# Attention on one core: where the fold of a head's halves stands in the ScalarE and VectorE queues

## The chip, the cores and the metric

The kernel runs on one core of one Trainium2 chip, as a single launch. The metric is the device time of that launch in microseconds (us). One core has five engines with an instruction queue each: TensorE (PE in the profile, with its weight loads as PEld), VectorE (DVE), ScalarE (ACT), GpSimd (POOL) and SyncE (SP), which here only issues DMAs.

## The reference, cut to what matters

Two layers of a transformer trunk over 1024 tokens of 1024 features, in float32. Each layer has an attention stage and a dense SwiGLU stage. The first layer (called A here) has windowed attention with 12 query heads, the second (B) a two-dimensional neighbourhood attention with 12; both have 4 more heads over 256 memory tokens.

```python
def reference(x, mem, ...):
    for i in range(DEPTH):                       # 2 layers
        h = rmsnorm(x, norm_mix[i])
        y_tok = windowed_gqa(...) if i % 2 == 0 else neighbourhood_attn(...)   # 12 heads of 64
        y_mem = memory_attn(qm, mk, mv)                                        # 4 heads of 64
        x = x + jnp.concatenate([y_tok, y_mem], axis=-1) @ w_out[i]
        h = rmsnorm(x, norm_ffn[i])
        gu = h @ w_gate_up[i]
        x = x + (jax.nn.silu(gu[..., :D_FF]) * gu[..., D_FF:]) @ w_down[i]
    return rmsnorm(x, norm_final)
...
    p = jax.nn.softmax(s)                        # in each head
    o = jnp.einsum('bkgniu,bnukd->bnikgd', p, vband)
```

## The kernel before

Every float32 operand of a matmul is kept as a high part, rounded to the matmul's type by ACT (`hi`, L107), and a low part, the rest, which DVE makes (`lo`, L110). Products are sums of such parts. In attention, a value tile holds a head's values as 64 high and 64 low columns side by side, so the product of probabilities and values comes out on 128 partitions: the upper 64 rows belong to the low part. To finish a head they have to be added to the lower 64. This is the fold: ACT copies the upper rows to a temporary `yt` (L819) and DVE adds the lower rows and `yt` into the result tile `y` (L830).

The attention stage works on "halves": one head (16 of them) and one half of the tokens (512, in four blocks of 128), so 32 halves per layer and 64 in all. For each half there are three jobs:

- `scores` (L739): per block two matmuls into a PSUM bank `S` (there are two such banks), a DVE pass that adds the bias and takes the row minimum (L757; for memory heads a maximum, L752), an exponential on ACT (L761 or L753); then a reciprocal on DVE (L769, L771) and the scaling of the four blocks by POOL (L774).
- `turn` (L782): per block two or three transposes on PE into a PSUM bank `pT` (L789; three banks, tag `T`), then `ph` on ACT (L793) and `pl` on DVE (L794), which are `hi` and `lo` of the transposed block. The fourth block of a half needs the bank of the first one, so its transposes wait for the first `pl`.
- `mix` (L797): the matmuls of `ph` and `pl` with the values (L809) into the PSUM bank `O`, and at its end the fold. There is one `O` bank (`ps_o`, one buffer), so the first L809 matmul of a half waits for the fold of the half before. At the second half of an odd head the finished pair of heads, `y`, is stored to `y_d` by a DMA on SP's queue (L832), and read back later (`load_y`, L938).

The main loop (L963 to L1000) traces, for each i, the scores of half i+1, the mix of half i-1 with its fold, and the turn of half i. Between the steps of these jobs it pulls pieces of other work: the projections of later heads (`mm`, L141), and towards the end of the stage the first pieces of the output projection (`po`, L141; `out_units`, L945). The last heads have only `po` to be filled with; these halves are called the tail here.

The order of the trace isn't yet the order in the queues. The Tile framework's scheduler goes through the traced instructions with that order as priority, and puts those first whose inputs and buffers its own cost model holds to be ready. Then each engine runs its queue in order. Semaphores are set where an instruction depends on one of another engine.

Of the kernel before, what the change touches and what calls it, by code (L numbers as in the profile page):

```python
# [41 lines left out]
def trunk_kernel(ctx: ExitStack, tc: tile.TileContext, a: dict, out: bass.AP):  # L42
# [17 lines left out]
    nc = tc.nc  # L60
# [37 lines left out]
    def temp(name="t2k", n=HS):  # L98
        t = phase[0].tile([P, HS], F32, tag="t2k", name=name, bufs=phase[1])
        return t[:, :n] if n != HS else t  # L100
# [3 lines left out]
        return phase[0].tile([P, D], F32, tag="raw", name=name, bufs=phase[2])  # L104

    def hi(dst, src):
        nc.scalar.copy(dst, src)  # L107

    def lo(dst, src, h, eng=None):
        (eng or nc.vector).tensor_tensor(dst, src, h.bitcast(F32), op=ALU.subtract)  # L110

    def load_w(src, tag="whl", bufs=3, eng=None, name="w", pool=wp, parts=1, raw=None):
        if raw is None:
# [33 lines left out]
    def run(g):  # L147
        for _ in g:
            pass
# [392 lines left out]
    for layer in range(2):  # L542
        is_a = layer == 0
        with tc.tile_pool(name=f"ap{layer}", bufs=1, reuse_waits="tile") as ap:
# [163 lines left out]
                return lambda qb: t[:, 1 if qb in (0, 7) else 0]  # L708


            biases, ys = {}, {}

            class Half:
                def __init__(self, h, u):
# [67 lines left out]
                def turn(self):  # L782
                    self.ph = ap.tile([P, 12, P], F32R, tag="ph", bufs=2, name="ph")
                    self.pl = ap.tile([P, 12, P], F32R, tag="pl", bufs=2, name="pl")
                    step = 4 if self.mem else 2
                    for p, (qb, b0, b1, n) in zip(self.p, self.blocks):
                        tr = ps_t.tile([P, HS], F32, tag="T", name="pT")
                        for j in range(b1 - b0):
                            nc.tensor.transpose(tr[:, j * P : (j + 1) * P], p[:, j * P : (j + 1) * P], ident)  # L789
                        s0 = self.slot(b0, qb)  # L790
                        sl = slice(s0, s0 + step * (b1 - b0 - 1) + 1, step)
                        src = tr[:, :n].rearrange("p (j q) -> p j q", q=P)
                        hi(self.ph[:, sl], src)  # L793
                        lo(self.pl[:, sl], src, self.ph[:, sl])  # L794
                        yield

                def mix(self):  # L797
                    u = self.u
                    if u == 0 and not self.odd:
                        ys[self.pair] = ap.tile([P, S], F32, tag="y", bufs=2, name="y")  # L800
                    y = ys[self.pair]
                    o = ps_o.tile([P, HS], F32, tag="O", name="O")
                    js = sorted({j for _, b0, b1, _ in self.blocks for j in range(b0, b1)})
                    for j in js:
                        qbs = [qb for qb, b0, b1, _ in self.blocks if b0 <= j < b1]
                        s0, w = self.slot(j, qbs[0]), len(qbs)
                        c0 = (qbs[0] - 4 * u) * P
                        for t in (self.ph, self.pl):
                            nc.tensor.matmul(  # L809
                                o[:, c0 : c0 + w * P], self.value(j),  # L810
                                t[:, s0 : s0 + w].rearrange("p j q -> p (j q)"),
                                start=j == js[0] and t is self.ph, stop=j == js[-1] and t is self.pl,
                                skip_group_check=True,
                            )
                        yield

                    t = temp("yt")
                    rs = slice(HD, P) if self.odd else slice(0, HD)
                    nc.scalar.copy(t[:HD], o[HD:])  # L819
                    if self.mem:  # L820
                        d, o_, t_ = y[rs, u * HS : (u + 1) * HS], o[:HD], t[:HD]
                    elif is_a:
                        v = lambda z: z.rearrange("p (r f c) -> p f r c", f=2, c=32)
                        d = y[rs].rearrange("p (f r c) -> p f r c", f=2, c=32)[:, :, 8 * u : 8 * u + 8]
                        o_, t_ = v(o[:HD]), v(t[:HD])
                    else:
                        v = lambda z: z.rearrange("p (s r c) -> p r s c", s=4, c=SC)
                        d = y[rs, u * HS : (u + 1) * HS].rearrange("p (r s c) -> p r s c", s=4, c=SC)
                        o_, t_ = v(o[:HD]), v(t[:HD])
                    nc.vector.tensor_tensor(d, o_, t_, op=ALU.add)  # L830
                    if u == 1 and self.odd and self.pair != last_pair:
                        nc.sync.dma_start(y_d[layer][self.pair], y)  # L832


            heads = [("m", 0), ("m", 1), *range(6), ("m", 2), ("m", 3), *range(6, NH)]
# [85 lines left out]
            def pull():  # L921
                try:
                    next(work)
                    taken[0] += 1
                except StopIteration:
                    pass
# [9 lines left out]
                yT[f][k] = t  # L936

            def load_y(f, k):  # L938
                raw = temp("yr")
                nc.sync.dma_start(raw, y_d[layer][k][:, f * HS : (f + 1) * HS])  # L940
                split_y(f, k, raw)
# [21 lines left out]
            for i in range(len(halves)):  # L963

                rate = 0.0
                for n in range(n0, len(units)):
                    if done[0] > n:
                        continue
                    left = (n + 1 - n0) * 2 * NK - taken[0]
                    rate = max(rate, left / max(dues[n] - i - 0.5, 0.5))  # L970
                if tail is not None:
                    rate = PACE[layer][i - len(halves)]
                if i == 0:
                    for _ in range(8):
                        pull()
                if is_a and 4 <= i < 4 + ROWS // 2:
                    for r in (2 * i - 8, 2 * i - 7):
                        spread_bias(r)
                jobs = []
                if i + 1 < len(halves):  # L980
                    jobs.append(halves[i + 1].scores())
                ahead = halves[min(i + 3, len(halves) - 1)].h
                if not isinstance(ahead, tuple) and ahead not in biases:
                    biases[ahead] = make_bias(ahead)
                if i > 0:
                    jobs.append(halves[i - 1].mix())
                jobs.append(halves[i].turn())
                for job in jobs:
                    for _ in job:
                        credit += rate / groups  # L990
                        while credit >= 1.0:
                            credit -= 1.0
                            pull()

                for n in range(n0, len(units)):
                    while dues[n] <= i + 1 and done[0] <= n:
                        pull()
                at[0] = i + 1
                if done[0] == len(units) and tail is None:
                    tail = work = out_units()  # L1000
            for _ in halves[-1].mix():
                pull()
            run(tail)
            for f in range(2):
                split_y(f, last_pair, ys[last_pair][:, f * HS : (f + 1) * HS])
# [731 lines left out]
```

## Time and profile before

| what | value |
|---|---|
| time, median of 3 runs | 2117.06 us (2116.92 to 2117.7) |
| time of the profiled execution | 2115.94 us |
| span of the profiled execution | 2114.2 us |
| DVE busy | 1524.6 us (72%) |
| ACT busy | 1077.9 us (51%) |
| POOL busy | 583.6 us (28%) |
| DMA, mean over the span | 136 GB/s |

The span is the time from the first to the last instruction in the trace; the time of an execution has 1.7 us around it. "Busy" is the share of the span in which an engine had at least one instruction running. A PE instruction's end is modelled, and one matmul starts while the one before still counts as running; so PE can be called busy while it waits for a short time. Such waits show in the distance from one start to the next.

In time, attention of layer A lies at about 80 to 335 us of the span and that of layer B at about 1060 to 1392 us; the tails begin at about 282 and 1364 us. The rest is the dense stage.

### The profile page before, as it was taken

Reading aid. Unit: us, or ns where it says so; the run is one execution under the profiler, and the core shown is the slowest. Engines: PE = TensorE matmul, PEld = TensorE weight load, DVE = VectorE, ACT = ScalarE, POOL = GpSimd, SP = SyncE. Lnnn points to the kernel's source line nnn. Section 1 sums busy time; section 2 is a strip of 40 time slices with the busy share of each in tenths; the row PEclk is TensorE's granted clock in tenths of the full one; section 3 lists DMA queues with packets and bytes.
Section 4 is the critical chain, followed back from the end, with each engine's and each line's share of the span. In section 5 each row is a group of like instructions: output and inputs, shape, how many; then the busy total and the mean of one; then the engine's idle time right before and its main releaser. Section 6 shows DMA issues by size and latency. Waiting matters only on the chain.

```text
span 2114.2 us, 29053 instructions
## 1 busy us (share of the span) xinstructions
PE 2092.7 (99%) x10318; PEld 1750.1 (83%) x10318; DVE 1524.6 (72%) x2474; ACT 1077.9 (51%) x2037; POOL 583.6 (28%) x615
## 2 busy tenths in 40 slices
PE   9999999999999999999999999999999999999998
PEld 8788888888888888888888888888888888888887
DVE  7687886987666667776766666677986666677675
ACT  6687775544434335344466666664543434344443
POOL 0344330334444430000233223203243444400001
PEclk9999999999999999999999999999999999999999
DMA  6421128332333227866232222275232333267662
GB/s 232 146 82 51 36 83 288 99 115 100 110 108 111 91 105 254 313 216 207 78 110 68 69 72 78 64 266 157 75 110 105 110 115 104 91 254 256 205 221 95
DMA packets 121778, 288.08 MB, mean 136 GB/s; under 512 B 12705, under 2 KB 21153, under 8 KB 121633
## 3 DMA queue, kind: packets, MB, share of 16 engines
q1 hardware_dynamic: 113744, 272.42, 38.4%
q10 hardware_dynamic: 7888, 13.79, 1.7%
q8 instruction: 82, 1.34, 0.3%
q14 instruction: 64, 0.52, 0.1%
HBM read 211.19 MB, written 68.95 MB: 133 GB/s over the span
## 4 chain that ended last, share of the span: by engine, by line
PE 80%; issue 12%; DVE 3%; ACT 2%; POOL 2%; DMA 1%; POOLq 0%; ACTq 0%; SPq 0%; DVEq 0%
PE X L1101 16%; PE Y L1101 16%; PE mm L141 15%; PE po L141 8%; PE X L1532 5%; PE Y L1532 4%; PE O L809 3%; PE S L746 3%; PE pT L789 3%; PE X L1183 2%; PE Y L1183 2%; PE mm L448 1%; ACT p L761 1%; POOL wS L1058 1%; POOL wf L110 1%
## 5 line engine op out<-in xcount | busy, mean ns | idle before, releaser
L1101 PE MATMUL Y<-hB,wgu 128*128 128x512 f32 x1056 | 255.5, 391 | 0.8 <-ACT c L1121 0.8
L1101 PE MATMUL X<-hB,wgu 128*128 128x512 f32 x1056 | 254.8, 391 | 0.0
L1532 PE MATMUL X<-hB,wd 128*128 128x512 f32 (+1 forms) x1092 | 243.2, 383 | 0.9 <-DVE x L1496 0.9
L110 DVE TENSOR_TENSOR wgu<-wS,wgu 128x1024 fp32r<-128x1024 f32 (+1 forms) x124 | 155.4, 1253 | 120.9 <-ACT wgu L107 120.7
L1532 PEld LDWEIGHTS X<-hB,wd 128*128 128x128 f32 x1092 | 200.2, 188 | 41.4 <-issue 1.7
L1101 PEld LDWEIGHTS Y<-hB,wgu 128*128 128x128 f32 x1056 | 196.8, 188 | 43.4 <-ACT c L1121 1.6
L1101 PEld LDWEIGHTS X<-hB,wgu 128*128 128x128 f32 x1056 | 196.0, 188 | 39.8
L774 POOL TENSOR_SCALAR p<-p,stat 128x384 f32<-128x384 f32 (+1 forms) x256 | 143.1, 579 | 308.7 <-DVE stat L771 213.4
L141 PE MATMUL mm<-hT,wqk 128*128 128x512 f32 x672 | 199.3, 405 | 0.0
L107 ACT CAST wgu<-wS 128x1024 fp32r<-128x1024 f32 (+1 forms) x124 | 114.3, 923 | 142.0 <-POOL wS L1058 124.6
L141 PE MATMUL po<-yT,wo 128*128 128x512 f32 x768 | 184.2, 393 | 0.0
L1532 PE MATMUL Y<-hB,wd 128*128 128x512 f32 x792 | 180.4, 389 | 0.0
L1532 PEld LDWEIGHTS Y<-hB,wd 128*128 128x128 f32 x792 | 148.6, 188 | 31.2 <-DVE x L1496 0.4
L244 POOL TENSOR_TENSOR nr<-nv,neg_half 128x4 f32<-128x4 f32 (+1 forms) x12 | 13.3, 1105 | 582.9 <-DVE nv L243 573.7
L141 PEld LDWEIGHTS po<-yT,wo 128*128 128x128 f32 x768 | 142.7, 188 | 28.8 <-DVE yT L110 0.2
L1101 PE MATMUL X<-hT,wgu 128*128 128x512 f32 x624 | 150.2, 391 | 0.0
L107 ACT CAST hB<-b_raw 128x512 fp32r<-128x512 f32 x154 | 89.4, 618 | 115.5 <-DMA b_raw<-b_d 100.3
L1058 POOL TENSOR_TENSOR wS<-wgu_raw 128x512 f32<-128x512 f32 x44 | 61.2, 1391 | 292.1 <-DVE wgu L110 292.1
L1101 PEld LDWEIGHTS X<-hT,wgu 128*128 128x128 f32 x624 | 116.8, 188 | 26.3
L761 ACT ACTIVATE p<-p,stat 128x256 f32<-128x256 f32 (+1 forms) x192 | 112.4, 587 | 48.1 <-DVE stat L757 46.0
L110 DVE TENSOR_TENSOR pl<-pT,ph 128x384 fp32r<-128x384 f32 (+1 forms) x256 | 119.0, 493 | 19.1 <-ACT ph L107 15.9
L110 DVE TENSOR_TENSOR hB<-b_raw,hB 128x512 fp32r<-128x512 f32 x154 | 99.9, 687 | 42.2 <-ACT hB L107 42.1
(201 smaller groups left out, 4248.1 us busy)
## 6 DMA issues: line engine op xcount, KB each, us to landing
wgu_raw<-in_w_gu SPq DMA_DIRECT2D x92, 512.0 KB, 3.7
wd_raw<-in_w_dn SPq DMA_DIRECT2D x70, 512.0 KB, 4.4
b_raw<-b_d SPq DMA_DIRECT2D x70, 512.0 KB, 5.4
b_d<-c SPq DMA_DIRECT2D x88, 256.0 KB, 2.1
b_d<-t SPq DMA_DIRECT2D x66, 256.0 KB, 2.2
wo_raw<-in_w_out SPq DMA_DIRECT2D x32, 512.0 KB, 3.5
xr_d<-x ACTq DMA_DIRECT2D x32, 256.0 KB, 2.5
xr<-xr_d SPq DMA_DIRECT2D x16, 512.0 KB, 6.1
```

Source lines behind the costliest of these rows:

```text
L107: nc.scalar.copy(dst, src)
L110: (eng or nc.vector).tensor_tensor(dst, src, h.bitcast(F32), op=ALU.subtract)
L141: nc.tensor.matmul(ps[:, :n], l, r, start=start and i == 0 and j == 0, stop=stop and i == len(order) - 1 and j == 2,)
L746: nc.tensor.matmul(s_[:, :n], Q[self.h][:, qb * P : (qb + 1) * P], k, start=j == 0, stop=j == 1)
L761: nc.scalar.activation(p[:, :n], p[:, :n], AF.Exp, bias=m1, scale=-1.0, accum_out=s1)
L774: nc.gpsimd.tensor_scalar(p[:, :n], p[:, :n], ri[:, i : i + 1], 1.0, op0=ALU.mult, op1=ALU.mult)
L789: nc.tensor.transpose(tr[:, j * P : (j + 1) * P], p[:, j * P : (j + 1) * P], ident)
L809: nc.tensor.matmul(o[:, c0 : c0 + w * P], self.value(j), t[:, s0 : s0 + w].rearrange("p j q -> p (j q)"), start=j == js[0] and t is self.p ...
L1058: sub = lambda o, p_, q_: nc.gpsimd.tensor_tensor(o, p_, q_, op=ALU.subtract)
L1101: nc.tensor.matmul(ps, l, r, start=n in (0, 1, 3, 6) and k == 0 and i == 0, stop=k == 3 and i == 2, skip_group_check=True,)
L1183: nc.tensor.matmul(bank[:, at : at + h2], l, r, start=start and k == 0 and i == 0, stop=stop and k == 1 and i == 2, skip_group_check=True,)
L1532: nc.tensor.matmul(bank[:, c], l, r, start=i in (0, 1, 3, 6) and p == 0 and n == 0, stop=p == HF - 1 and n == 2, skip_group_check=True,)
```

## The change

The fold is taken out of `mix` and becomes a method of its own, `fold`. The main loop calls it for half i-1 after the turn of half i, not before it. All that it traces is put into a context in which each traced instruction gets an order edge, without a semaphore, behind the last `ph` of the turn (if it runs on ACT) or the last `pl` (if on DVE). So the copy may not stand ahead of the four `ph` in ACT's queue, nor the add ahead of the four `pl` in DVE's. The store of `y` moves with it. The last half's fold has nothing to stand behind. An assertion makes sure that a pair is stored before it is read back.

```diff
@@ helpers
     def hi(dst, src):
-        nc.scalar.copy(dst, src)
+        return nc.scalar.copy(dst, src)
     def lo(dst, src, h, eng=None):
-        (eng or nc.vector).tensor_tensor(dst, src, h.bitcast(F32), op=ALU.subtract)
+        return (eng or nc.vector).tensor_tensor(dst, src, h.bitcast(F32), op=ALU.subtract)
@@ class Half, turn
-                        hi(self.ph[:, sl], src)
-                        lo(self.pl[:, sl], src, self.ph[:, sl])
+                        self.last = hi(self.ph[:, sl], src), lo(self.pl[:, sl], src, self.ph[:, sl])
                         yield
@@ class Half, end of mix
-
+                    self.o = o
+
+                def fold(self, behind=None):
+                    u, y, o = self.u, ys[self.pair], self.o
                     t = temp("yt")
                     rs = slice(HD, P) if self.odd else slice(0, HD)
+                    with ExitStack() as queued:
+                        for ins in behind.last if behind else ():
+                            queued.enter_context(tc.issue_after(ins.ins))
+                        self.add_halves(t, rs, u, y, o)
+                    if u == 1 and self.odd and self.pair != last_pair:
+                        nc.sync.dma_start(y_d[layer][self.pair], y)
+                        stored.add(self.pair)
+
+                def add_halves(self, t, rs, u, y, o):
                     nc.scalar.copy(t[:HD], o[HD:])
...
                     nc.vector.tensor_tensor(d, o_, t_, op=ALU.add)
-                    if u == 1 and self.odd and self.pair != last_pair:
-                        nc.sync.dma_start(y_d[layer][self.pair], y)
@@ load_y
+                assert k in stored
@@ main loop, after the jobs of half i
+                if i > 0:
+                    halves[i - 1].fold(halves[i])
...
             for _ in halves[-1].mix():
                 pull()
+            halves[-1].fold()
```

The queues outside the two attention stages stay as they were. Three places follow, first of before and then of the change. Tiles have a number behind their name here; the changed file's lines are shifted (L808 is L809 of before, L830 is L819, L841 is L830).

**Place 1, ACT, the steady part of layer A.** O_2076 belongs to the second half of head 3; the four `ph` behind it are those of the first half of head 4. Before:

```order
L767 ACTIVATE stat_2038<-stat_2038,sink_108 128x4
L107 CAST QS_1961<-scaled_2090 64x16x32
L107 CAST KH_1962<-scaled_2090 64x16x32
L819 COPY yt_2108<-O_2076 64x512
L107 CAST ph_2112<-pT_2114 128x2x128
L107 CAST ph_2112<-pT_2119 128x3x128
L107 CAST ph_2112<-pT_2128 128x3x128
L107 CAST ph_2112<-pT_2134 128x3x128
L761 ACTIVATE p_2144,stat_2140<-p_2144,stat_2140 128x256
```

The same place with the change:

```order
L767 ACTIVATE stat_2038<-stat_2038,sink_108 128x4
L107 CAST QS_1961<-scaled_2090 64x16x32
L107 CAST KH_1962<-scaled_2090 64x16x32
L107 CAST ph_2108<-pT_2110 128x2x128
L107 CAST ph_2108<-pT_2115 128x3x128
L107 CAST ph_2108<-pT_2124 128x3x128
L107 CAST ph_2108<-pT_2130 128x3x128
L830 COPY yt_2136<-O_2076 64x512
L761 ACTIVATE p_2144,stat_2140<-p_2144,stat_2140 128x256
```

The copy moved from ahead of the four `ph` to behind them; the casts of a projection (QS, KH) still stand ahead, and the next exponentials stand behind in both.

DVE at this place, before:

```order
L110 TENSOR_TENSOR KL_1963<-scaled_2090,KH_1962 64x16x32
L830 TENSOR_TENSOR y_1785<-O_2076,yt_2108 64x2x256
L110 TENSOR_TENSOR pl_2113<-pT_2114,ph_2112 128x2x128
L110 TENSOR_TENSOR pl_2113<-pT_2119,ph_2112 128x3x128
L110 TENSOR_TENSOR pl_2113<-pT_2128,ph_2112 128x3x128
L757 ISA p_2144,stat_2140<-S_2141,bias_1942,nsink_109 128x256
L757 ISA stat_2140 128x1
L110 TENSOR_TENSOR pl_2113<-pT_2134,ph_2112 128x3x128
```

With the change:

```order
L110 TENSOR_TENSOR KL_1963<-scaled_2090,KH_1962 64x16x32
L110 TENSOR_TENSOR pl_2109<-pT_2110,ph_2108 128x2x128
L110 TENSOR_TENSOR pl_2109<-pT_2115,ph_2108 128x3x128
L110 TENSOR_TENSOR pl_2109<-pT_2124,ph_2108 128x3x128
L110 TENSOR_TENSOR pl_2109<-pT_2130,ph_2108 128x3x128
L841 TENSOR_TENSOR y_1785<-O_2076,yt_2136 64x2x256
L757 ISA p_2144,stat_2140<-S_2141,bias_1942,nsink_109 128x256
```

The add moved behind the four `pl`, and now stands ahead of all L757 passes of the next scores; before, one of them came ahead of the last `pl`.

**Place 2, PE at the same place**, from the transposes of the first half of head 4 to the first matmul of its O. Before:

```order
L789 MATMUL pT_2128<-ident_106,p_1971 128x128 x3
L746 MATMUL S_2141<-KH_1012,QS_1344 128x256
L746 MATMUL S_2141<-KL_1013,QS_1344 128x256
L141 MATMUL mm_2104<-hT_586,wqk_1499 128x512 x2
L789 MATMUL pT_2134<-ident_106,p_1977 128x128 x3
L141 MATMUL mm_2104<-hT_586,wqk_1499 128x512
L746 MATMUL S_2150<-KH_1012,QS_1344 128x384
L746 MATMUL S_2150<-KL_1013,QS_1344 128x384
L141 MATMUL mm_2104<-hT_624,wqk_1499 128x512 x3
L746 MATMUL S_2156<-KH_1012,QS_1344 128x384
L746 MATMUL S_2156<-KL_1013,QS_1344 128x384
L809 MATMUL O_2179<-ph_2112,V_833 128x256
```

With the change:

```order
L789 MATMUL pT_2124<-ident_106,p_1971 128x128 x3
L789 MATMUL pT_2130<-ident_106,p_1977 128x128 x3
L746 MATMUL S_2141<-KH_1012,QS_1340 128x256
L746 MATMUL S_2141<-KL_1013,QS_1340 128x256
L141 MATMUL mm_2104<-hT_586,wqk_1499 128x512 x3
L746 MATMUL S_2150<-KH_1012,QS_1340 128x384
L746 MATMUL S_2150<-KL_1013,QS_1340 128x384
L141 MATMUL mm_2104<-hT_624,wqk_1499 128x512 x3
L141 MATMUL mm_2104<-hT_629,wqk_1499 128x512
L808 MATMUL O_2179<-ph_2108,V_833 128x256
```

The transposes of the fourth block moved up to those of the third, and more other matmuls stand between the last transpose and the first matmul of the next O.

**Place 3, ACT in the tail of layer A.** O_3485 is that of the first half of head 9, and the four `ph` are those of its second half. Before:

```order
L107 CAST ph_3499<-pT_3501 128x3x128
L107 CAST ph_3499<-pT_3507 128x3x128
L761 ACTIVATE p_3457,stat_3453<-p_3457,stat_3453 128x256
L761 ACTIVATE p_3463,stat_3453<-p_3463,stat_3453 128x384
L819 COPY yt_3496<-O_3485 64x512
L761 ACTIVATE p_3469,stat_3453<-p_3469,stat_3453 128x384
L761 ACTIVATE p_3475,stat_3453<-p_3475,stat_3453 128x384
L767 ACTIVATE stat_3453<-stat_3453,sink_108 128x4
L107 CAST ph_3499<-pT_3513 128x3x128
L107 CAST ph_3499<-pT_3519 128x2x128
```

With the change:

```order
L107 CAST ph_3496<-pT_3498 128x3x128
L761 ACTIVATE p_3457,stat_3453<-p_3457,stat_3453 128x256
L107 CAST ph_3496<-pT_3504 128x3x128
L107 CAST ph_3496<-pT_3510 128x3x128
L761 ACTIVATE p_3463,stat_3453<-p_3463,stat_3453 128x384
L761 ACTIVATE p_3469,stat_3453<-p_3469,stat_3453 128x384
L761 ACTIVATE p_3475,stat_3453<-p_3475,stat_3453 128x384
L767 ACTIVATE stat_3453<-stat_3453,sink_108 128x4
L107 CAST ph_3496<-pT_3516 128x2x128
L830 COPY yt_3521<-O_3485 64x512
```

Here the copy stood between two exponentials; now it stands behind all of them and behind the last `ph`.

More of the change, by code (lines that the diff above doesn't have):

```diff
@@ L708, in make_bias @@
                 return lambda qb: t[:, 1 if qb in (0, 7) else 0]
-            biases, ys = {}, {}
+            biases, ys, stored = {}, {}, set()
             class Half:
```

## The prediction

> **What bounds the kernel now.** I read the page first (busy shares, slices, granted clock), then busy time in four stretches, then who waits for whom, then the timeline around single folds. The page first:
>
> ```profile
> span 2114.2 us, 29053 instructions
> ...
> PE 2092.7 (99%) x10318; PEld 1750.1 (83%) x10318; DVE 1524.6 (72%) x2474; ACT 1077.9 (51%) x2037; POOL 583.6 (28%) x615
> ...
> PEclk9999999999999999999999999999999999999999
> ```
>
> PE is busy for all but 21.5 us of the span, with its full clock in every slice. An engine that is busy for 72% or 51% costs nothing by itself; the change can only win what PE loses to waits in the two attention stages. These are the steady part and the tail of layer A, then of layer B (columns: stretch and length, then busy us of PE, PEld, DVE, ACT, POOL):
>
> ```profile
> 80.00:262.00 182.00, 179.06 (x1009) 150.48 (x1007) 141.65 (x370) 137.72 (x374) 76.82 (x133) 1.00 0.19 60
> 262.00:335.00 73.00, 71.83 (x392) 59.31 (x391) 60.14 (x142) 56.54 (x132) 18.14 (x30) 1.00 0.40 140
> 1060.00:1364.00 304.00, 303.60 (x1639) 256.11 (x1637) 197.11 (x471) 194.42 (x486) 96.36 (x154) 1.00 0.25 73
> 1364.00:1392.00 28.00, 27.51 (x157) 23.12 (x156) 21.24 (x49) 20.07 (x46) 6.03 (x11) 1.00 0.58 190
> ```
>
> PE is idle for 2.9 + 1.2 + 0.4 + 0.5 = 5.0 us of these 587. What for, by the waits of PE's matmuls in 80 to 335 us, and by those of the whole span for the two instructions of the fold (total, times, longest):
>
> ```profile
> PE pT L789 <- DVE pl L110: 2.7, 7, 0.8
> ...
> DVE y L830 <- ACT yt L819: 37.4, 38, 3.2
> ACT yt L819 <- PE O L809: 35.0, 30, 2.8
> ```
>
> The two big numbers, 37.4 and 35.0 us, are idle time of ACT and DVE at the head of their queues, and not the gain: neither engine is the bound. They count only where what stands behind them makes PE late, and that is the 2.7 us: transposes that wait for a `pl` to free one of the three pT banks. This is how it comes about, at place 1:
>
> ```profile
> 172.90 0.86 PE L141 MATMUL mm<-hT,wqk 128*128 128x512 f32 x3
> 173.60 0.71 PE L789 MATMUL pT<-ident,p 128*128 128x128 f32 x5
> 174.06 0.94 PE L141 MATMUL mm<-hT,wqk 128*128 128x512 f32 x3
> 174.18 0.59 ACT L819 COPY yt<-O 64x512 f32<-64x512 f32 x1
> 174.49 0.96 DVE L110 TENSOR_TENSOR KL<-scaled,KH 64x512 fp32r<-64x512 f32 x1
> 174.79 1.14 ACT L107 CAST ph<-pT 128x256 fp32r<-128x256 f32 x3
> 175.41 0.62 PE L141 MATMUL mm<-hT,wqk 128*128 128x512 f32 x2
> 175.49 0.68 DVE L830 TENSOR_TENSOR y<-O,yt 64x512 f32<-64x512 f32 x1
> 176.20 1.35 DVE L110 TENSOR_TENSOR pl<-pT,ph 128x256 fp32r<-128x256 f32 x3
> 176.77 0.52 PE L789 MATMUL pT<-ident,p 128*128 128x128 f32 x3 [0.74 <-DVE pl L110]
> ```
>
> The first transposes are done at about 174, but ACT makes yt first, then DVE makes y, and only then the first `pl`; the fourth block's transposes start at 176.77. Two more things are in these rows. Three matmuls of 512 columns take 0.86 us together and one alone 0.39, so they start every 0.23 us: of each wait behind one, 0.16 us doesn't show as idle. And five transposes take 0.71, one 0.27: they start every 0.11 us, but a matmul follows the last of them after 0.03.
>
> **What goes: the waits for a pT bank.** I went through the start times of PE's matmuls and took each transpose that starts over 0.12 us later than its usual distance, 0.15 us behind the end of a `pl` that a fold had delayed. There are 10 in layer A (4.7 us) and 3 in B (0.8 us). The first and the last, each with the matmuls ahead:
>
> ```profile
> 135.98 0.48 PE L141 MATMUL mm<-hT,wqm 128*128 128x512 f32 x1
> 136.65 0.41 PE L789 MATMUL pT<-ident,p 128*128 128x128 f32 x2 [0.19 <-DVE pl L110]
> ...
> 1331.00 0.86 PE L141 MATMUL mm<-hT,wv 128*128 128x512 f32 x3
> 1332.04 0.41 PE L789 MATMUL pT<-ident,p 128*128 128x128 f32 x2 [0.18 <-DVE pl L110]
> ```
>
> The first: 136.65 - 135.98 - 0.23 = 0.44 us. The last: the third matmul starts at 1331.47, so 0.34. Together 5.5 us, the upper bound; the lower is the idle that the view itself shows, 2.7.
>
> With the change, yt (0.58) and y (0.68) leave their place ahead of the first `pl`, which comes some 0.7 us earlier. Most of these waits are shorter than that. Place 1 gains nothing, though: there KL still stands ahead of `pl` (until 175.45), so the bank comes free 0.73 us earlier, but PE arrives earlier too, since two S matmuls and two mm (0.03 + 2 x 0.12 + 2 x 0.23, about 0.7 us) no longer stand ahead of the fourth transposes. Its 0.89 us stay. Of the largest wait, at 260 us (1.0 us), I leave 0.3 for the same reason. 5.5 - 0.9 - 0.3 = 4.3; I take **-4.2 us**.
>
> **What comes: O waits for the fold.** Now the copy starts behind the last `ph` and the add behind the last `pl`, and the one O bank is free only then. The lengths of this chain, from a half without other work in the way, and of the fold's two instructions (min/median/max):
>
> ```profile
> 144.54 0.52 PE L789 MATMUL pT<-ident,p 128*128 128x128 f32 x3
> 145.13 0.28 PE L746 MATMUL S<-KH,QS 128*128 128x256 f32 x1
> 145.24 0.28 PE L746 MATMUL S<-KL,QS 128*128 128x256 f32 x1
> 145.36 0.34 PE L746 MATMUL S<-KH,QS 128*128 128x384 f32 x1
> 145.53 0.34 PE L746 MATMUL S<-KL,QS 128*128 128x384 f32 x1
> ...
> 145.09 0.48 ACT L107 CAST ph<-pT 128x384 fp32r<-128x384 f32 x1 [0.40 <-PE pT L789]
> ...
> 146.55 0.61 DVE L757 CUSTOM_DVE_ANT_0 p<-S,bias,nsink 128x384 f32<-128x384 f32 x1
> ...
> L819 ACT COPY yt<-O x64: 567/584/587, 93.4 to 1387.6; 64x512 f32<-64x512 f32 x64
> L830 DVE TENSOR_TENSOR y<-O,yt x64: 669/683/687, 94.4 to 1388.2; 64x512 f32<-64x512 f32 x64
> ...
>   DVE pl L110: 2.5, 9
>   ACT ph L107: 1.7, 6
>   DVE y L830: 0.9, 3
> ```
>
> The last transpose starts at 144.79, `ph` 0.30 later; 0.48 for `ph`, 0.58 for yt, 0.68 for y, and 0.1 for the hops between: 2.14 us until O may be written again (2.03 where the last block has two tiles and `ph` takes 0.37). Against that stands the work that PE has between the last transpose and the next O. At place 2 it is now 0.03 for the step from the transposes, 2 x 0.12, 3 x 0.23, 2 x 0.17 and 4 x 0.23 = 2.2 us: just enough; before it was 1.6. Counted like this in all 64 halves: in the steady part of A 1.9 to 2.6 us, in a few more (0.5 to 2.7 before), where six halves are short by 0.1 to 0.2, 0.8 us in all; in the steady part of B 2.6 to 4.7, none short. In A's tail, ACT has more ahead of the last `ph`: at place 3 three exponentials and the sink's, so some 0.5 us there, and in the half before a cast of wo, 0.4 to 1.0. I take 1.3 for A's tail and 0.6 for B's last four halves. Where O waits, the add is late for DVE's next work as well: all L757 passes (0.61 each) now stand behind it, and the third S matmul waits for the first of them, since S has two banks. I give that 0.7. Sum 3.4 us; from below it is nothing, if all chains are as clean as the one shown, from above 0.3 us in each of the 24 steady halves of A and 0.6 in each of the 12 of the tails, 14 us.
>
> Off this goes what O's matmuls and their weight loads wait for today, `pl`, `ph` and y: 2.5 + 1.7 + 0.9 in the rows above, in which idle of weight loads is counted that a running matmul covers; I take 1.5. Net **+1.9 us**.
>
> **What moves beside it.** Counted in the two orders, 584 transposes directly follow another one, 577 before; each costs 0.11 in place of 0.03: **+0.6 us**. The stores of y move back with their folds, and SP runs its queue in order, so the read-backs behind one come later:
>
> ```profile
> 266.36 0.33 SPq L832 DMA_DIRECT2D y_d<-y  x1
> 266.78 0.38 SPq L940 DMA_DIRECT2D yr<-y_d  x1
> ...
> 271.48 0.62 ACT L107 CAST yT<-yr 128x512 fp32r<-128x512 f32 x1 [0.54 <-DMA yr<-y_d]
> 273.40 0.62 ACT L761 ACTIVATE p<-p,stat 128x384 f32<-128x384 f32 x1 [1.29 <-DVE stat L757]
> ```
>
> The store would go some 3 us later, and the cast that waits for the read-back with it, to 274.5. In the changed ACT queue that cast stands behind the exponential of 273.40, which isn't done before 274.0. So the later data are hidden by that; without the cover ACT would stand 3 us longer, beside 5 us of PE's work in that half. I put it at nothing, 0 to 3. No semaphore comes with the order edges, and nothing outside attention is reordered.
>
> The sum is -4.2 + 1.9 + 0.6 = **-1.7 us**. The profiled execution took 2115.94 us (span 2114.2 and 1.7 around it), 1.1 less than the median of the runs, 2117.06. From the median the forecast is **2115.4 us**.
>
> **The rivals.** (1) *The single O bank becomes the bound*, slower. In each half PE waits for the fold, as it now has 2.1 us to hide behind just as much work. For it: the chain has no slack in A, and casts of 1 us lie about in ACT's queue. Against it: in B there are 3 to 4 us of cover, and PE's row of waits names y in 0.9 us only. If 24 steady halves lose 0.2 us and 12 tail halves 0.4 beyond my count, that is 9.6 more: 2125 us. It decides from 0.16 us per half in these 36 (1.7 + 4.2 = 5.9 us). The Trainium skill has a rule on this side ("PSUM — Partial Sum Buffer", the summary's rules for kernel authors): evacuate PSUM promptly. By it, the time would grow by this mechanism; that each half's O bank is now held longer is clear from the queues, while the rows of B, where PE has other work, show no price for it.
>
> (2) *The pT wait only changes place.* The transposes of the fourth block moved up in PE's queue, as at place 1, so PE arrives earlier and waits as long. If only 1.4 of the 5.5 us go, the sum is 2.8 worse: 2118.2 us. For it: place 1 itself, the wait of 0.89 us. Against it: the other waits are mostly 0.2 to 0.45, below the 0.7 us by which `pl` comes earlier.
>
> (3) *More goes than I count*: all 5.5 us, 1.9 of O's waits, and no new ones: -7, 2110 us. For it: the scheduler has put just the missing work ahead of O. Against it: PE shows 5.0 us idle in all.
>
> That the change doesn't do what it says is excluded by the queues, which show the fold behind the turn.
>
> **How the numbers follow.** The forecast with its neighbours (2113 to 2117.6) gets 0.45, rival 2 (up to 2121) 0.22, rival 3 0.18, rival 1 0.15. About 0.2%, or 4.2 us, is what a measurement of this kernel can tell from no change. Faster by more: rival 3 and a rim of the forecast, 0.24; slower by more: rival 1 and a little, 0.16; within: 0.60. The range reaches into rivals 1 and 3 until half of each is left out, 0.16: 2110.5 to 2122.
>
> **What would show it.** Right: PE's wait of pT for `pl` falls from 2.7 us to about 1; ACT's wait of yt for O (35.0) nearly goes; PE, or its weight loads, waits for y in place of `pl` and `ph`, 2 to 4 us in all, mostly in A; the stretch from 80 to 335 us is 1 to 3 us shorter, B's the same within 1. Wrong: waits of O for y above 6 us (rival 1); pT's wait for `pl` as before (rival 2); the tail of A longer by over 3 us; or a difference in the dense stage, where the queues are the same.

## The result, and the profile after

The changed kernel takes 2122.18 us (median of 7 runs, 2121.35 to 2126.61) against 2117.06 (7 runs, 2115.7 to 2117.7): a ratio of 1.0028, 95% interval 1.0018 to 1.0038. It is 5.1 us slower. The forecast was 2115.4, with a range that ended at 2122.0. The profiled execution took 2121.91 us.

First the page of the changed kernel, then its waits over the whole span (total, times, longest), in the rows that answer to those shown of before:

```profile
span 2120.1 us, 29001 instructions
...
PE 2095.9 (99%) x10318; PEld 1748.7 (82%) x10318; DVE 1526.4 (72%) x2474; ACT 1078.9 (51%) x2037; POOL 582.7 (27%) x615
```

```profile
PE pT L789 <- DVE pl L110: 4.9, 10, 0.8
...
DVE y L841 <- ACT yt L830: 5.9, 15, 2.4
ACT yt L830 <- PE O L808: 3.7, 2, 2.5
```

Before, the first of these rows was, over the whole span:

```profile
PE pT L789 <- DVE pl L110: 2.8, 8, 0.8
```

The fold no longer waits at the head of the two queues: the add's 37.4 us have become 5.9, the copy's 35.0 have become 3.7. But the transposes wait longer for `pl`, not shorter: 4.9 us in place of 2.8. (Line numbers moved: the copy is L830, the add L841, O's matmuls L808.)

Where in time the loss lies is read from TensorE's own work. Each layer's attention runs from its first score matmul to its last output-projection matmul. The view by tile gives these (min/median/max, then start of the first and of the last), for layer A and then layer B. Before:

```profile
L746 PE MATMUL S<-mKH,QS x32: 277/283/387, 76.1 to 216.9; 128*128 128x256 f32 x32
L141 PE MATMUL po<-yT,wo x384: 387/389/486, 279.3 to 393.4; 128*128 128x512 f32 x192
...
L746 PE MATMUL S<-mKH,QS x32: 275/281/366, 1062.4 to 1250.8; 128*128 128x256 f32 x32
...
L141 PE MATMUL po<-yT,wo x384: 387/389/486, 1363.9 to 1466.1; 128*128 128x512 f32 x192
```

With the change:

```profile
L746 PE MATMUL S<-mKH,QS x32: 274/286/386, 75.5 to 218.1; 128*128 128x256 f32 x32
...
L141 PE MATMUL po<-yT,wo x384: 387/389/486, 280.6 to 393.8; 128*128 128x512 f32 x192
...
L746 PE MATMUL S<-mKH,QS x32: 277/282/385, 1064.3 to 1255.2; 128*128 128x256 f32 x32
...
L141 PE MATMUL po<-yT,wo x384: 387/389/488, 1368.8 to 1472.1; 128*128 128x512 f32 x192
```

Layer A went from 393.4 - 76.1 = 317.3 to 318.3 us, **+1.0**. Layer B went from 1466.1 - 1062.4 = 403.7 to 407.8, **+4.0** (4.02 before rounding). The dense stage between them, whose queues the change leaves alone, took 1.5 us more in this execution; more on it below. So four fifths of the attention's loss lie in layer B, for which the forecast had nothing beyond its tail.

What TensorE waits for there, by the waits of its weight loads in 1060 to 1364 us. Before:

```profile
PEld S L746 <- DVE stat L757: 2.7, 11, 0.4
PEld S L746 <- ACT p L753: 1.1, 5, 0.2
PEld vtr L596 <- ACT vT L639: 0.9, 4, 0.2
```

With the change:

```profile
PEld S L746 <- DVE stat L757: 4.3, 14, 0.4
PEld S L746 <- ACT p L753: 2.1, 8, 0.5
PEld vtr L596 <- ACT vT L639: 1.3, 4, 0.5
PEld O L808 <- DVE y L841: 0.8, 2, 0.6
```

The score matmuls wait 1.6 us more for the passes that free a score bank, and 1.0 us more for the exponentials that free one in memory heads. O's wait for the fold is the smaller part, 0.8 us. (A weight load's wait can be covered in part by a matmul that still runs. And the window is fixed: moved with the layer, to 1064.3 to 1368.8 us, the passes' row of the change reads 4.9.) One such place shows how it comes about, in the timeline, before and after. Before:

```profile
1228.79 0.89 DVE L110 TENSOR_TENSOR pl<-pT,ph 128x384 fp32r<-128x384 f32 x2 [0.46 <-ACT ph L107]
...
1229.59 0.41 DVE L752 TENSOR_REDUCE stat<-S 128x1 f32<-128x256 f32 x1
...
1230.10 0.47 ACT L753 ACTIVATE p<-S,stat 128x256 f32<-128x256 f32 x1 [1.07 <-DVE stat L752]
```

With the change:

```profile
1232.45 0.89 DVE L110 TENSOR_TENSOR pl<-pT,ph 128x384 fp32r<-128x384 f32 x2 [0.46 <-ACT ph L107]
...
1232.72 0.58 ACT L830 COPY yt<-O 64x512 f32<-64x512 f32 x1
...
1233.37 0.68 DVE L841 TENSOR_TENSOR y<-O,yt 64x512 f32<-64x512 f32 x1
...
1233.83 1.32 PE L141 MATMUL mm<-hT,wv 128*128 128x512 f32 x5
1234.09 0.76 DVE L752 TENSOR_REDUCE stat<-S 128x1 f32<-128x256 f32 x2
...
1234.61 0.47 ACT L753 ACTIVATE p<-S,stat 128x256 f32<-128x256 f32 x1 [1.30 <-DVE stat L752]
...
1235.22 0.19 PEld L746 LDWEIGHTS S<-mKH,QS 128*128 128x128 f32 x1 [0.50 <-ACT p L753]
```

Before, the first pass starts 0.80 us after the last `pl` pair has begun, 1229.59 - 1228.79. Now the add stands between them, and it is 1.64 us. There are two score banks, so the third block's scores need what follows this pass, the exponential; their weight load waits 0.50 us for it, behind five matmuls of a projection (three before). Before the change the add ran ahead of the four `pl`, where VectorE had time: that is what its 37.4 us of waiting were.

### The profile page after: what moved, and what is told of

The parts are those of the page before. It is cut to its first block, busy times and chain, and to the rows that moved or that the text cites. A ratio compares the mean times of both kernels' runs of the same rounds, so it can differ in the third digit from the quotient of the medians.

```text
span 2120.1 us, 29001 instructions
## 1 busy us (share of the span) xinstructions
PE 2095.9 (99%) x10318; PEld 1748.7 (82%) x10318; DVE 1526.4 (72%) x2474; ACT 1078.9 (51%) x2037; POOL 582.7 (27%) x615
## 4 chain that ended last, share of the span: by engine, by line
PE 78%; issue 12%; DVE 5%; ACT 3%; POOL 2%; DMA 1%; POOLq 0%; SPq 0%; ACTq 0%; DVEq 0%
PE X L1114 16%; PE Y L1114 16%; PE mm L141 13%; PE po L141 8%; PE X L1545 5%; PE Y L1545 4%; PE S L746 3%; PE O L808 3%; PE pT L789 3%; PE X L1196 2%; PE Y L1196 2%; PE mm L448 1%; ACT p L761 1%; POOL wS L1071 1%; POOL wf L110 1%
## 5 line engine op out<-in xcount | busy, mean ns | idle before, releaser
L107 ACT CAST ph<-pT 128x384 fp32r<-128x384 f32 (+1 forms) x256 | 103.6, 435 | 81.2 <-PE pT L789 79.4
```

What stands on the lines that cost most here:

```text
L107: return nc.scalar.copy(dst, src)
```

## The experiments

Two theories ran through most of them. **D**: the add stands on VectorE straight ahead of the next passes, so score banks come free late. **O** (rival 1 of the prediction): the one O bank is held longer. A third, **N**, put the loss down to transfers in the dense stages. In each kernel the scheduler also places TensorE's other work anew, so no run moves the fold alone. The table has, of each kernel's one profiled execution against that of before, how much longer layer A, the dense stage between the layers, and layer B took (us, by the rows above). The ratio is from all runs, with its 95% interval.

| kernel | A | between | B | median us (before beside it) | ratio |
|---|---|---|---|---|---|
| the change | +1.0 | +1.5 | +4.0 | 2122.18 (2117.06) | 1.0028 (1.0018 to 1.0038) |
| e1 layer A only | +1.1 | +4.7 | +0.3 | 2122.2 (2118.26) | 1.0015 (1.0006 to 1.0024) |
| e2 layer B only | +0.2 | +1.2 | +3.8 | 2121.51 (2118.26) | 1.0015 (1.0006 to 1.0024) |
| e3 add behind first pass | -0.7 | +2.8 | +3.2 | 2121.11 (2118.26) | 1.0013 (1.0004 to 1.0021) |
| e4 add behind second pass | -2.5 | +2.8 | +1.9 | 2118.04 (2118.26) | 1.0002 (0.9993 to 1.0011) |
| e5 only the add held | +1.8 | +1.2 | +2.2 | 2123.29 (2117.35) | 1.003 (1.0018 to 1.0041) |
| e6 no order | +1.1 | +3.0 | +0.8 | 2119.79 (2117.35) | 1.0009 (1.0001 to 1.0018) |
| e7 e4 in A, before in B | -2.7 | +1.4 | +0.1 | 2115.14 (2117.35) | 0.9988 (0.9979 to 0.9997) |
| e8 short add | -2.0 | +2.1 | +2.5 | 2117.74 (2117.35) | 0.9999 (0.999 to 1.0008) |
| e9 late add, free copy | -1.6 | +0.2 | +1.4 | 2117.18 (2118.15) | 0.9998 (0.9989 to 1.0006) |
| e10 short add, free copy | +0.7 | +1.7 | +2.5 | 2121.29 (2118.15) | 1.0015 (1.0006 to 1.0024) |
| e11 the change again | +1.1 | +0.8 | +4.4 | 2124.17 (2118.15) | 1.0031 (1.0019 to 1.0043) |
| e12 e7 again | -2.1 | +3.7 | +0.1 | 2116.09 (2118.27) | 0.9989 (0.998 to 0.9998) |

**One layer at a time.** The main loop gets two places for the fold, and each layer takes one:

```diff
+                place = 3 if is_a else None          # e2: None if is_a else 3
...
+                    if what == "mix" and place is None:
+                        halves[i - 1].fold()         # where it was, nothing held
+                if i > 0 and place == 3:
                     halves[i - 1].fold(halves[i])
```

> The move is kept in layer A; in layer B the fold is traced where it was, without the order. Theory D (the add now stands on VectorE straight ahead of the next half's score passes, so that score banks come free late, and it took layer B's loss from this): layer B reads as before, PEld's waits of S for the passes and exponentials about 3.8 us in 1060-1364 against 6.4 with the whole change, and the time is 2117 to 2118.5 us. Theory O (the one bank of O, held longer, is what costs, in both layers): about half of the loss stays, 2119.5 us. Theory N (the loss is a shift of transfers in the dense stages, not of the attention): 2122 us, as with the whole change.

> The move is kept in layer B alone; layer A is as before. Theory D: the loss of layer B is there in full, 3.5 to 4.5 us, so 2120.5 to 2121.5 us, with PEld's waits of S in 1060-1364 at about 6.4 us and those of O under 1.5 us. Theory O: O's waits for y are the larger, over 3 us, and the time is 2119.5. Theory N: the time does not add up with that of the kernel that moves layer A alone; the two sums of differences miss 5 us by over 2.

By layer they come out as D expected: the moved layer shows the change's loss (+1.1 in A, +3.8 in B) and the other stays (+0.3 and +0.2). In e1 the waits of S in layer B are 2.5 + 1.1 us again, in e2 they are 4.8 + 2.1. The totals went otherwise: that of e1 is 2122.2 where D gave at most 2118.5, and it is the number of theory N. The two losses against before, 3.9 and 3.3 us, exceed the change's 5.1 by 2.1, which N had also named as its sign. In e1's profile the excess does lie between the layers (+4.7), where its queues are those of before. So the dense stage can move the total by nearly as much as the change does, and nothing about the attention could be read from it; that the attention loses what the moved layer shows rests on the two profiles, and on the repeat at the end.

**The add one and two passes later.** It is traced inside the scores of the half after the next, and held behind a pass of that half. The copy stays behind the last `ph`:

```diff
                         for ins in behind.last if behind else ():
                             queued.enter_context(tc.issue_after(ins.ins))
+                        if past:
+                            queued.enter_context(tc.issue_after(past.seen.ins))   # a pass
...
+                        if i > 1 and i + 1 < len(halves) and z == 0 and n == late:  # 0 or 1
+                            halves[i - 2].fold(halves[i - 1], halves[i + 1])
```

> As the change, but the add (and with it the copy's tracing) stands one score pass later: behind the first of the four passes of the half after the next, instead of straight behind the last pl. The next half's S of block 2 needs only that first pass, so theory D expects the waits of S in 1060-1364 to fall from 6.4 us to 4 or less, and the time to come back by 2 us or more, to 2118 to 2120 us. Theory O expects the opposite: O is held some 0.55 us longer per half, its waits for y grow by 3 us or more over both layers, and the time is 2124 to 2128 us.

> The same, two score passes later (some 1.1 us). Theory D: waits of S in 1060-1364 at 4 us or less, as with one pass, since the add now stands ahead of the passes that nobody waits for as urgently; O's waits for y grow, mostly in layer A where the span from the last transpose to the next O is 1.9 to 2.6 us; about 2119 to 2123 us. Theory O: 2130 us or more, O's waits for y over 10 us in both layers.

One pass later was not enough: S waits 6.3 us in 1060 to 1364 (3.8 and 0.5 for the passes, 2.0 for the exponentials), and D's numbers for e3 (4 us or less, 2118 to 2120 us) fell; so did O's (2124 us or more), and O's waits for y went down. Two passes later the waits are as D had them, and the time, 2118.04, is below D's range. e4, waits of the weight loads in the same stretch:

```profile
PEld S L746 <- DVE stat L757: 2.1, 8, 0.4
PEld S L746 <- ACT p L753: 1.8, 8, 0.3
...
PEld O L808 <- DVE y L843: 0.3, 1, 0.3
```

3.9 us, as before the change (3.8). D's reading is that with two score banks two passes are urgent, and an add ahead of either delays the next score matmuls. It fits e3 and e4; e5, below, limits it. Layer B's loss is halved and layer A turns into a gain of 2.5 us. Theory O can't hold for e4: the bank is held longer still, from the start of a half's last O matmul to the end of its fold 5.6 us on average over 27 halves of layer A, 5.0 with the change, 2.6 before. Yet O's waits for y, 3.1 us in layer A with the change, fall to 0.3 in 80 to 335 us, as the scheduler also put the next half's O matmuls later (6.0 us behind the last ones on average, 5.3 with the change). The prediction weighed a rule of the Trainium skill here ("PSUM — Partial Sum Buffer", the summary's rules for kernel authors: evacuate promptly). Taken as a rule on time, e4 should have been slower than the change and e3; its ratio is 1.0002, theirs are 1.0028 and 1.0013.

**Copy and add apart.** e5 drops the order from the copy, e8 shortens the add to one eighth of its columns (217 ns in place of 683; it leaves out the rest of attention's output), e10 does both, e9 lets the copy free and has the add late. e6 drops the order altogether:

```diff
-                        for ins in behind.last if behind else ():
+                        for ins in behind.last[1:] if behind else ():    # e5, e10: the add only
...
-                    nc.vector.tensor_tensor(d, o_, t_, op=ALU.add)
+                    nc.vector.tensor_tensor(d[cut], o_[cut], t_[cut], op=ALU.add)   # e8, e10
...
-                    halves[i - 1].fold(halves[i])
+                    halves[i - 1].fold()                                 # e6
```

> As the change, but only the add is held behind the last pl; the copy on ScalarE may go as early as the scheduler puts it, as before the change. The stretch of layer B's attention (1060 to 1395 us by the same matmuls) is 4.0 us longer with the whole change. Theory D (the add on VectorE ahead of the score passes): it stays 3 us longer or more, with PEld's waits of S for the passes at 4 us or more in 1060-1364 (2.7 before, 4.3 with the change). Theory C (the copy, now on ScalarE straight ahead of the next exponentials, is what costs): it falls to 1.5 us or less, and the waits of S for the exponentials go from 2.1 back to 1.1 us.

> The fold is traced behind the next half's transposes, as in the change, but without the order that holds it there; the scheduler puts the add back near its old place in most halves. Theory D: no loss in layer B over 1 us, waits of S for the passes at 3 us or less in 1060-1364, and the time 2116 to 2119 us. If it is the place in the trace that costs (the y stores and the O bank's release traced later), 2121 to 2123 us as with the change.

> As the change, but the add computes only one eighth of its columns (64 instead of 512; the rest of y is set to zero on GpSimd when y is made, so the attention's output is left out but for an eighth). The add then holds VectorE for some 0.15 to 0.25 us instead of 0.69. Theory D: waits of S for the passes fall from 4.3 us to 3 or less in 1060-1364, and layer B's attention is at most 2 us longer than before (4.0 with the change). Theory C or a cost of the order on TensorE alone: it stays 3 us longer or more.

> The add stands behind the second score pass of the half after the next, and the copy is not held at all. If the loss of layer B is two parts that add up (the add ahead of the first two score passes, some 1.5 us; the copy behind the last ph and so ahead of the exponentials and of vT's copies, some 2 us), both are gone here: layer B's attention is at most 1.2 us longer than before (4.0 with the change, 1.9 with the add late and the copy held), PEld's waits in 1060-1364 are at most 3 us for the score passes, 1.3 for the exponentials and 1.0 for vT. If the loss is the O bank held longer (theory O), it is 3 us or more, since O is held longest here. Layer A as with the late add, 2 to 3 us shorter than before, or up to 1 us less than that. Time 2115 to 2118.5 us.

> The add held behind the last pl but computing one eighth of its columns (the rest of y set to zero, the output left out but for an eighth), the copy free. With the two kernels that do one of these, it completes the square: layer B's attention is 4.0 us longer than before with the whole change, 2.2 with the copy free, 2.5 with the add short. If copy and add cost apart from each other, this one is 0.4 to 1.2 us longer than before; if the one only costs by delaying the other (the add waits for the copy), it stays at 2 us or more.

In layer B, freeing the copy takes 1.8 us off (e5) and shortening the add 1.5 (e8), but both together no more (e10: +2.5). So neither theory of e5 held alone, and the sum of parts that e9 and e10 were to test isn't a sum. e5 speaks against D as it was put. The add stands where the change has it, behind a `pl` and ahead of two passes in 26 of layer B's 32 halves (25 with the change), and D had expected 4 us or more of waits for the passes. In 1060 to 1364 us they are:

```profile
PEld S L746 <- DVE stat L757: 2.0, 8, 0.4
PEld O L808 <- issue: 1.6, 3, 0.7
```

That is less than before the change (with the window moved along, 2.6 us, about as before). What is new there is O's: TensorE's O matmuls wait 0.5 us for y, and each of the three waits called "issue" ends 0.12 us behind the end of an add. So theory O, out for e4, holds for part of e5's loss. In sum the add's place alone doesn't lengthen the waits for the passes, though at the place shown above the weight load still waits 0.51 us; with the copy held as well it does (4.3).

With the copy free the waits for exponentials and for vT go back to those of before. e9, in 1060 to 1364 us:

```profile
PEld S L746 <- DVE stat L757: 3.1, 10, 0.7
...
PEld S L746 <- ACT p L753: 1.1, 5, 0.3
PEld vtr L596 <- ACT vT L639: 0.9, 4, 0.2
```

So what the change adds to these last two rows is the held copy's, which ScalarE then makes ahead of the next half's exponentials and of vT. e9's first row is a little over what was expected (3), and so is the 1.4 us that it left in layer B (1.2).

e8, too, ended between the two theories, with 3.2 us of waits for the passes (3 expected) and +2.5 in B (2 expected). Why so little came back shows at the place above. In e8:

```profile
1231.43 0.22 DVE L843 TENSOR_TENSOR y<-O,yt 64x64 f32<-64x64 f32 x1
...
1231.67 0.84 DVE L752 TENSOR_REDUCE stat<-S 128x1 f32<-128x256 f32 x2
...
1231.88 0.86 PE L141 MATMUL mm<-hT,wv 128*128 128x512 f32 x3
...
1232.81 0.19 PEld L746 LDWEIGHTS S<-mKH,QS 128*128 128x128 f32 x1 [0.50 <-ACT p L753]
```

The first pass starts 0.48 us sooner behind the last `pl` pair than with the full add, but the scheduler put three matmuls of the projection there in place of five, so TensorE arrives sooner as well, and the weight load waits as long as with the full add. In e10 this place looks the same, with three matmuls and 0.51 us. Its waits for the passes, 3.6 + 0.5 us, hold another one, 299 us into the layer:

```profile
1361.67 0.68 DVE L110 TENSOR_TENSOR yT<-yr,yT 128x512 fp32r<-128x512 f32 x1
1362.27 0.55 DVE L757 CUSTOM_DVE_ANT_0 p<-S,bias 128x384 f32<-128x384 f32 x1
...
1362.88 0.45 PE L746 MATMUL S<-KH,QS 128*128 128x384 f32 x1 [0.50 <-DVE stat L757]
```

Here it isn't the add that stands between the last `pl` and the first pass but `yT`, the low part of a pair read back for the output projection; the weight load waits 0.92 us for that pass and the matmul 0.50. The order is the same with the change and in e3, e5, e6 and e8; before the change, this `yT` stood ahead of the `pl`.

Without the order (e6), the scheduler puts most adds back ahead of the `pl`; layer B loses 0.8 us, waits for the passes are 3.0 + 0.4 us, a little over what was expected, and so is the time, 2119.79.

In layer A the held copy is a gain, in each of the three pairs that differ by it: +1.0 against +1.8 with the add behind the last `pl`, -2.0 against +0.7 with the short add, -2.5 against -1.6 with the late add. And the change gives it away again: e4, with the add and the fold's place in the trace later, is 3.5 us shorter there than the change.

**A better version.** e7 takes e4's place in layer A and that of before in layer B; e12 is the same kernel once more.

> In layer A the add stands behind the second score pass of the half after the next (which made layer A's attention 2.7 us shorter than before between 80 and 335 us); in layer B the fold is as before the change. If the layers are independent of each other, as the two kernels with one layer each suggest, layer A's attention is 2 to 3.5 us shorter than before, layer B's within 0.5 us of before, and the time is 2114 to 2116.5 us where before reads 2117 to 2118.3. Rival: layer A's gain is given back in the dense stage behind it, 2117 to 2119 us.

> The kernel with the late add in layer A and the old place in layer B once more. If its gain is the attention's and not a chance of the runs, layer A from its first score matmul to its last output-projection matmul is 2.2 to 3.2 us shorter than before, layer B within 0.5 us of it, and the time 1.5 to 3.5 us below that of before measured beside it. If it was chance, the ratio's interval holds 1 well inside it, and layer A is within 1 us of before.

Layer A is 2.7 and 2.1 us shorter (2.2 was the least expected of e12), layer B within 0.1 us. Both intervals end below 1: 0.9988 (0.9979 to 0.9997) and 0.9989 (0.998 to 0.9998), some 2.4 us faster than before the change.

**The change again**, beside e9 and e10:

> The whole change once more, on the chip of these runs. If the loss sits in the attention and not in a chip or a run, layer A's attention (80 to 335 us) is 0.6 to 1.6 us longer and layer B's (1060 to 1395) 3.5 to 4.5 us longer than before, and the time is 2120.5 to 2123.5 us. If the dense stages make it, the two stretches add up to less than 4 us.

+1.1 in A and +4.4 in B, as expected; the median, 2124.17, is 0.7 above the range given, and 6.0 above that of before beside it.

## Why the prediction was wrong

Two steps failed: the gain from the pT bank, which didn't come, and the price of the delayed score passes and exponentials, which was put at 0.7 us and came out at 2.6 in layer B's steady part alone.

**The waits for a pT bank go (-4.2): fell.** They grew, over the whole span from 2.8 to 4.9 us, in the view of 80 to 335 us from 2.7 to 3.8:

```profile
PE pT L789 <- DVE pl L110: 3.8, 8, 0.8
...
PEld O L808 <- DVE y L841: 3.1, 10, 0.7
```

It went as rival 2 had it. Up to 280 us it is 2.9 for 2.7; behind that, in A's tail, 0.8 for none, and as much in B's. At one place the timeline shows both causes. Before:

```profile
239.68 1.15 PE L789 MATMUL pT<-ident,p 128*128 128x128 f32 x9
...
241.06 0.68 DVE L830 TENSOR_TENSOR y<-O,yt 64x512 f32<-64x512 f32 x1 [0.23 <-ACT yt L819]
...
241.66 1.47 DVE L110 TENSOR_TENSOR pl<-pT,ph 128x384 fp32r<-128x384 f32 x3
242.35 0.41 PE L789 MATMUL pT<-ident,p 128*128 128x128 f32 x2 [0.24 <-DVE pl L110]
```

With the change:

```profile
240.61 1.17 PE L789 MATMUL pT<-ident,p 128*128 128x128 f32 x9
...
241.49 0.28 ACT L767 ACTIVATE stat<-stat,sink 128x4 f32<-128x4 f32 x1
...
242.00 0.18 DVE L769 RECIPROCAL stat<-stat 128x4 f32<-128x4 f32 x1
242.31 1.49 DVE L110 TENSOR_TENSOR pl<-pT,ph 128x384 fp32r<-128x384 f32 x3
243.01 0.41 PE L789 MATMUL pT<-ident,p 128*128 128x128 f32 x2 [0.53 <-DVE pl L110]
```

The fold is gone from ahead of the first `pl`, but exponentials, the sink's and the reciprocal still are: from the first transposes to the fourth block's it is 2.40 us, 2.67 before. So the bank comes free 0.27 us earlier where the prediction had counted 0.7. TensorE meanwhile lost two score matmuls and one of a projection from ahead of those transposes and so arrives earlier and waits longer, idle for 0.53 in place of 0.24 us. The prediction had seen this at its place 1, and granted it to two of 13 places.

**O waits for the fold (+1.9 net): its mechanism held.** The new waits were put at 3.4 us; in A the weight loads and matmuls wait 3.1 + 0.3 for y, in B's steady part 0.8. The old ones, for `pl` and `ph`, nearly go, and more than the 1.5 taken off. The signs named for the fold's own waits came out nearly: the copy's wait went (35.0 to 3.7), and over the whole span O waits 4.2 + 0.3 us for y, where 2 to 4 were named.

**The passes behind the add (0.7, a part of that term): the mis-sized one.** The prediction saw that all L757 passes now stand behind the add, and that the third score matmul waits for the first. But it priced this only where O waits as well, and called layer B covered. It needs no wait of O: the add stands ahead of these passes in most halves. And for the copy, which now stands ahead of exponentials and of vT on ScalarE, the sum has no term at all. In B's steady part S alone waits 2.6 us more (4.3 + 2.1 for 2.7 + 1.1), 1.6 for the passes and 1.0 for the exponentials, and vT's transposes 0.4. Up to its output projection's first matmul, with the same matmuls ahead of it, B lost 2.9 of its 4.0 us. Behind it (from 1368.8 us, 1363.9 before) lies the tail, for which 0.6 was taken for O; it lost 1.1. The rows that grew there are those of the transposes (0.8 us for `pl`, none before; weight loads 2.1 for POOL's `p`, 1.1 before), not those of O. Shown is that these waits come with the fold's new place and go with it (e1, e2, e4, e7); how they divide between add and copy isn't, as e5, e8 and e10 don't add up.

**More transposes in a row (+0.6)** was not tested by itself. **The read-backs on SP (0)**: no row of the waits of `po` has grown, 0.2 us for each operand before and after. But in layer B one `yT` of a read-back has got between the last `pl` and the first pass, and the score matmuls' weight load waits 0.54 us there with the change.

**The signs named.** "B the same within 1" was the sign that failed most clearly. The dense stage's difference was named as a sign against the account as well, and it did differ, by 1.5 us in the profiled execution. In 795 to 815 us (waits before):

```profile
ACT hB L107 <- DMA b_raw<-b_d: 3.9, 3, 1.8
```

and with the change:

```profile
ACT hB L107 <- DMA b_raw<-b_d: 5.6, 3, 2.8
```

A load came later there. The "between" column shows +0.2 to +4.7 us over kernels that have the same order in that stage, so this is not put down to the change. All of them lie above the one profile of before, whose execution was itself 1.1 us under its median; whether the moved attention has a part in that isn't shown.

**Open**: the 1.4 us that layer B still loses with the add late and the copy free; how the 2.5 us of the short add with a free copy divide; and how much of the spread between the layers follows from when attention ends.

## What to carry to other kernels

An instruction that waits at the head of an in-order queue costs nothing where the engine has nothing better to do; moved out of that gap, it stands in front of something else and can delay it by its full duration. Ask of its new place what follows it in the queue, and how many buffers the consumers of that have: here, with two score banks and the copy held, the waits of the score matmuls were back where they had been only with the add behind the second pass. And price such a delay in every iteration, not only in those where another wait is seen. A kernel whose queues a scheduler fills can hide what an experiment takes away: with the add cut to a third of its time, the scheduler left less other work in between, and the wait stayed.

## What the runs showed of the hardware beyond this

One kernel's runs spread over more than the whole effect: before itself ran from 2114.46 to 2121.26 us in the 22 runs beside e9 to e11. In the dense stage between the layers, with unchanged queues, the profiled executions differ by up to 4.7 us (none in before itself, +0.2 in e9, +4.7 in e1). Attention, read layer by layer from the starts of TensorE's matmuls, repeated within 0.4 us where the queues were those of before (layer B of e1, e7 and e12: +0.3, +0.1, +0.1; layer A of e2: +0.2) and where the change was run twice (+1.0 and +1.1, +4.0 and +4.4); between e7 and e12 layer A differs by 0.6. A difference of 1 us in a stage could be read there that no median of the whole could show.
